# Five more Strassen groups, and the attention filled with parts of twenty of them

## The chip, the cores and the metric

The kernel runs on one core of one Trainium2 chip. Its time is that of the device for one execution, in microseconds (us). The core has a matrix engine (PE, with its weight loads shown as PEld), three engines for elementwise work (DVE, ACT and POOL) and a queue, SP, from which nearly all transfers are issued.

## What is computed

One layer of a hybrid backbone over 1024 tokens of 1024 channels. The normed and modulated input h is multiplied by one wide matrix; the columns of the product feed three branches, and each branch ends in a gate:

```python
z = h @ lp['w_in']                       # 1024 x 8704, used here from column 1536 on as 56 tiles of 128
ya = neighbourhood_attention(q, k, v, kc, vc, rpb) * silu(z[..., A_Z:B_B])
yb = bg * dw_conv(cg * val, w_conv3) * silu(gz)            # short convolution, 3 taps
u  = dw_conv(a * sigmoid(g), w_conv31) + b_conv            # 31 taps
yc = silu(layer_norm(u)) * silu(z[..., C_Z:GATES])
ga, gb, gc = split(sigmoid(z[..., GATES:]), 3)
m = ga * (ya @ w_out_a) + gb * (yb @ w_out_b) + gc * (yc @ w_out_c)
x = x + gate * (m @ w_o)
```

All is computed in float32 accuracy: each factor is split into a high and a low part, and a product takes three matmuls (high by high, high by low, low by high).

## The kernel before

Channels lie on the partitions, tokens on the free axis. A *channel tile* is 128 of the columns of z: `ZA`, `BG`, `CG`, `BV`, `BZ`, `CA`, `CGL`, `CZ` have four each, the gates `GT` twenty-four. h is kept split, as `hlf[half][k]`: eight rows k of 128 channels, two halves of 512 tokens, each with its high and low part. (`hcols` cuts columns from it.)

**A whole tile** (`plain`, lines 642 to 652) takes its weight row of 1024 in three pieces (`load_w`: a load on SP, a cast on ACT for the high part, a difference on POOL for the low part) and then 2 halves x 8 rows x 3 = 48 matmuls of 512 columns. ACT evicts the bank with a tanh (or, for a gate, a sigmoid); DVE makes the silu; a store takes it to DRAM.

**A Strassen group** (`group`, lines 803 to 836) makes two channel tiles at once with seven products instead of eight (Winograd's form): the weights of the two tiles are four blocks a11, a12, a21, a22 of 512 columns, h is four blocks B11, B12, B21, B22 (four rows by one half), and a product is 4 x 3 = 12 matmuls. Sums of weight blocks s1 to s4 are made on POOL (for the b groups partly on DVE, by `few`); the sums T1, T2, T3 and T4 of blocks of h are made in advance by `h_sums`, go through DRAM (`td`) and are loaded and split by `load_t`. T4 lies where B12 lay, in `hlf[1][0..3]`. The products in order are P1 = a11 B11 (bank ga), s2 T2 (gf), s1 T1 (gc), s3 T3 (gd), then a12 B21 added onto P1 in ga, which gives the first quarter C11 of the result, s4 B22 (ge), and a22 T4 added onto gd. DVE adds the products up: u2, v, then the quarters C22, C12, C21 (`add`). A bank to which a second product is added must first have been read. `run` interleaves: the last product of a group comes behind the first two products of the next.

**The long convolution** (`conv_steps`, lines 754 to 772) is done by DVE while PE makes the groups: 4 channel tiles x 31 taps x 2 halves, each tap a multiply-add of 512 columns onto a PSUM bank. `conv_step(n)` puts n taps at places in the groups (4 and 3 per group). After a tile's 31st tap ACT evicts it, and then the next tile's first tap may run.

**Order of the work.** The kernel names an order; a planner then walks the program with a model of the engines and puts on each engine's queue whatever is ready, what stands earlier in the program first. Each engine works its queue in that fixed order. `issue_after` forces an instruction behind another. Work that stands late in the program is so drawn forward to where PE waits for the attention.

The stages: the start and the first q, k, v (to about 110 us), the attention of eight heads (to 495 us) whose waits PE fills with q, k, v of the next heads, `glu` and then eight whole tiles (ZA and BZ, `plain`, lines 687 to 690); a bridge of two whole gate tiles after the attention's last product (lines 739 to 741) while the T blocks are loaded; 17 groups (to 845 us: four times b_start, a gate pair, b_end, then five of CZ and gates); `last_two`, two groups made together; then the merge of the branches (`merge`), the layer norm beside it, and the output product.

## Time and profile before

| | |
|---|---|
| median of 3 executions | 1102.34 us (1101.36 to 1103.52) |
| the profiled execution | 1105.51 us |
| its span, first to last instruction | 1103.6 us |
| PE busy | 1078.2 us, 5330 matmuls |
| DVE busy | 802.5 us |
| POOL busy | 628.0 us |
| ACT busy | 535.2 us |
| mean granted clock of PE | 0.99 |

Busy times are a union: overlapping instructions of an engine count once. Matmuls overlap, so the duration shown for one is longer than the time it adds. Rows of groups read: line, engine, operation, out<-in by the names of tiles, partitions x elements, count | busy us, mean ns of one | idle time of the engine before them and what ended it. Rows of windows give, for a stretch of the span, each engine's busy time with its number of instructions, then the granted clock, the share of the 16 DMA engines and GB/s.

### The profile page before, as it was taken

To read this page: it belongs to the slowest core of one execution; us is meant where nothing else is said; L and a number is where in the kernel's file an instruction comes from. 1 tells how busy PE (TensorE), PEld (TensorE's weight loads), DVE (VectorE), ACT (ScalarE), POOL (GpSimd) and SP (SyncE) were. 2 spreads that over 40 slices of the span, in tenths; PEclk is the share of its full clock that TensorE was granted. 3 is DMA by queue.
4 is the path that set the end of the run, shared out by engine and by line. 5 is a ranking of instruction groups with operands and counts; after the bars stand their busy time and mean duration, and the time that the engine had idled before them with its cause. 6 is when DMAs were issued, how large, how long until landed. Compare 5 with 4: busy or idle time off the path is not lost.

```text
span 1103.6 us, 15912 instructions
## 1 busy us (share of the span) xinstructions
PE 1078.2 (98%) x5330; PEld 923.4 (84%) x5330; DVE 802.5 (73%) x1379; ACT 535.2 (48%) x1138; POOL 628.0 (57%) x634
## 2 busy tenths in 40 slices
PE   6899999999999999999999999999999999999998
PEld 5788998998999888888888788888888888887886
DVE  6985577666766765536996898799794469889664
ACT  6765666667566655535223233333334344356630
POOL 3244967437536952213858677777778381493670
PEclk8899999999999999999999999999999999999999
DMA  9627523303213332119133433434344998372262
GB/s 350 220 77 249 179 60 117 111 34 104 94 66 86 108 122 77 63 43 352 34 130 105 135 114 119 149 106 163 123 143 177 375 363 303 120 244 77 96 223 101
DMA packets 79745, 163.17 MB, mean 148 GB/s; under 512 B 10320, under 2 KB 31440, under 8 KB 79568
## 3 DMA queue, kind: packets, MB, share of 16 engines
q1 hardware_dynamic: 75056, 160.06, 42.1%
q10 hardware_dynamic: 4608, 2.10, 0.7%
q8 instruction: 42, 0.69, 0.3%
q14 instruction: 39, 0.32, 0.1%
HBM read 120.18 MB, written 44.50 MB: 149 GB/s over the span
## 4 chain that ended last, share of the span: by engine, by line
PE 82%; POOL 6%; DMA 5%; issue 3%; DVE 1%; ACT 1%; SPq 1%; ACTq 0%; POOLq 0%; DVEq 0%
PE zaps L108 3%; PE zaps L109 3%; PE zaps L110 3%; PE py L609 3%; PE gd L791 3%; PE gd L793 3%; PE gd L792 3%; PE pp L589 3%; PE ga L791 3%; PE ga L793 3%; PE ga L792 3%; PE ps L108 3%; PE ps L110 3%; PE ps L109 3%; PE ops L108 3%
## 5 line engine op out<-in xcount | busy, mean ns | idle before, releaser
L767 DVE SCALAR_TENSOR_TENSOR cv<-upad,cf_t,cv 128x512 f32<-128x512 f32 x240 | 166.8, 744 | 0.1
L708 POOL TENSOR_TENSOR wl<-s,wh 128x512 fp32r<-128x512 f32 x69 | 93.3, 1364 | 15.9 <-ACT wh L707 15.1
L707 ACT CAST wh<-s 128x512 fp32r<-128x512 f32 x92 | 56.2, 617 | 92.4 <-POOL s L711 64.7
L91 POOL TENSOR_TENSOR wl<-wr,wh 128x384 fp32r<-128x384 f32 (+1 forms) x57 | 56.1, 992 | 72.2 <-ACT wh L89 61.5
L592 DVE TENSOR_TENSOR plo<-pp,phi 128x256 fp32r<-128x256 f32 (+2 forms) x96 | 54.3, 575 | 26.6 <-ACT phi L591 25.7
L708 POOL TENSOR_TENSOR wl<-wr,wh 128x512 fp32r<-128x512 f32 x44 | 60.8, 1382 | 4.3 <-ACT wh L707 4.2
L548 POOL TENSOR_TENSOR bias<-mk,img 64x96 f32<-64x96 bf16 (+1 forms) x96 | 45.8, 484 | 24.3 <-DVE mn L574 16.5
L591 ACT CAST phi<-pp 128x256 fp32r<-128x256 f32 (+2 forms) x96 | 46.4, 495 | 24.0 <-PE pp L589 23.4
L791 PE MATMUL ga<-ha,wh 128*128 128x512 f32 x148 | 57.6, 389 | 0.0
L792 PE MATMUL ga<-ha,wh 128*128 128x512 f32 x148 | 57.6, 389 | 0.0
L793 PE MATMUL ga<-ha,wl 128*128 128x512 f32 x148 | 57.6, 389 | 0.0
L575 ACT ACTIVATE pt<-sc,mn 128x256 f32<-128x256 f32 x64 | 30.5, 477 | 45.6 <-DVE mn L574 43.7
L574 DVE CUSTOM_DVE_ANT_0 pt<-sl,bias,mn 128x384 f32<-128x384 f32 (+1 forms) x64 | 37.2, 582 | 16.8 <-PE sl L571 15.7
L589 PE MATMUL pp<-ident,pt 128*128 128x128 f32 x304 | 47.0, 272 | 0.0
L79 POOL TENSOR_SCALAR ssh<-ssh 128x4 f32<-128x4 f32 (+1 forms) x40 | 11.4, 285 | 60.0 <-DVE ssh L228 57.2
L817 POOL TENSOR_TENSOR s<-wr 128x512 f32<-128x512 f32 x16 | 23.3, 1455 | 37.4 <-DMA wr<-in_wz 25.8
L89 ACT CAST wh<-wr 128x384 fp32r<-128x384 f32 (+1 forms) x66 | 31.4, 487 | 27.3 <-PE zaps L109 13.0
L589 PEld LDWEIGHTS pp<-ident,pt 128*128 128x128 f32 x304 | 38.0, 140 | 7.8
L978 ACT ACTIVATE c<-c 128x512 f32<-128x512 f32 x18 | 11.4, 632 | 63.9 <-DVE c L797 48.2
L708 POOL TENSOR_TENSOR wl<-wro,wh 128x512 fp32r<-128x512 f32 x12 | 17.1, 1428 | 42.5 <-ACT wh L707 31.4
L582 DVE TENSOR_SCALAR pt<-pt,mn 128x640 f32<-128x640 f32 (+1 forms) x64 | 40.0, 667 | 1.0
L80 POOL TENSOR_TENSOR ssh<-ssh,half_neg 128x4 f32<-128x4 f32 (+1 forms) x40 | 38.9, 974 | 3.0
(439 smaller groups left out, 3886.4 us busy)
## 6 DMA issues: line engine op xcount, KB each, us to landing
wr<-in_wz SPq DMA_DIRECT2D x34, 512.0 KB, 3.9
gs<-gd SPq DMA_DIRECT2D x24, 512.0 KB, 4.7
wada<-in_w_ada SPq DMA_DIRECT2D x16, 512.0 KB, 8.6
wrf<-in_wo SPq DMA_DIRECT2D x16, 512.0 KB, 3.6
cht<-chd SPq DMA_DIRECT2D x24, 256.0 KB, 3.2
wr<-in_wz SPq DMA_DIRECT2D x32, 192.0 KB, 2.4
wro<-in_wout SPq DMA_DIRECT2D x24, 256.0 KB, 5.3
gd<-gate SPq DMA_DIRECT2D x22, 256.0 KB, 3.3
```

The lines of the kernel that those rows point to most:

```text
L91: lo_eng.tensor_tensor(out=lo[:, :n], in0=raw[:, :n], in1=hi[:, :n].bitcast(F32), op=ALU.subtract)
L108: pe.matmul(ps, ah, bh, start=i == 0, stop=False)
L109: pe.matmul(ps, ah, bl, start=False, stop=False)
L110: pe.matmul(ps, al, bh, start=False, stop=i == n - 1)
L589: pe.transpose(out=pp[:, c * P : c * P + P], in_=src, identity=ident)
L592: dve.tensor_tensor(out=lo, in0=v, in1=hi.bitcast(F32), op=ALU.subtract)
L707: act.copy(hi, src)
L708: eng.tensor_tensor(out=lo, in0=src, in1=hi.bitcast(F32), op=ALU.subtract)
L767: dve.scalar_tensor_tensor(out=acc[b], in0=src, scalar=cf_t[:, i, j : j + 1], in1=acc[b], op0=ALU.mult, op1=ALU.add)
L791: pe.matmul(ps, wh, bh, start=first and j == 0, stop=False, skip_group_check=True)
L792: pe.matmul(ps, wh, bl, start=False, stop=False, skip_group_check=True)
L793: pe.matmul(ps, wl, bh, start=False, stop=last and j == 3, skip_group_check=True)
```

## The change

- `plain` is gone. The tiles ZA, BZ and the last two gates, ten in all, are now Strassen groups as well: a `plan` lists 22 groups (two BZ pairs, four b_start, four gate pairs, four b_end, two CZ pairs, two ZA pairs, four more gate pairs), before `last_two`.
- Of 20 of these (all but numbers 0 and 10) the two products on ga, P1 and a12 B21, are made ahead by `first_quarters`, with the whole weight row of the pair's first tile: 16 beside the attention, 4 in the bridge. P1 is copied out (`p1d`), then C11: as silu for ZA and BZ, raw into `gd` for gates (the sigmoid follows in `merge`), raw into `c11d` for the rest.
- In the group itself such a number loads P1 (and C11) and makes five products. Six conv taps stand in it, eight in a whole group.
- T4 is loaded and split beside the attention, before the fillers, into the place of B12, which no filler reads any more.
- A tap of the long convolution is one instruction of 1024 columns over two banks.
- ZA and BZ quarters made in groups get their silu from a sigmoid on ACT and a product on DVE (`twice_silu`).
- The loads and sums for group 0 (a BZ pair) are made early, with two splits ahead instead of one. Raw weight rows have four buffers instead of three. One product of b_end moves from DVE to POOL where C11 was made ahead.

```diff
+    plan = list(pairs())
+    whole_groups = (0, 10)
+    ahead_of = [n for n in range(len(plan)) if n not in whole_groups]
...
-        def plain(ct, dst, gate=False):
...
+        def quarter_part(part, n, w, ps):
+            for k in range(4 * part, 4 * part + 4):
+                wh, wl = w[k]
+                bh, bl = hcols(0, k, B512[0]), hcols(1, k, B512[0])
+                pe.matmul(ps, wh, bh, start=k == 0, stop=False, skip_group_check=True)
+                pe.matmul(ps, wh, bl, start=False, stop=False, skip_group_check=True)
+                pe.matmul(ps, wl, bh, start=False, stop=k % 4 == 3, skip_group_check=True)
+            kind, i, _ = plan[n]
+            t = tmp("quarter")
+            if part == 0:
+                p1d[n] = dst = dram.tile([P, 512], F32, name=f"p1d{n}")
+                act.copy(t, ps)
+            elif kind in ("za", "bz"):
+                dst = (zad if kind == "za" else zbd)[i][:, B512[0]]
+                act.activation(t, ps, AF.Tanh, scale=0.5)
+                dve.scalar_tensor_tensor(out=t, in0=t, scalar=1.0, in1=ps, op0=ALU.add, op1=ALU.mult)
+            else:
+                if kind == "gate":
+                    raw_gates.add(i)
+                    dst = gd[i][:, B512[0]]
+                else:
+                    c11d[n] = dst = dram.tile([P, 512], F32, name=f"c11d{n}")
+                act.copy(t, ps)
+            nc.sync.dma_start(dst, t)
...
-        for i in range(4):
-            plain(ZA + i, zad[i])
-        for i in range(4):
-            plain(BZ + i, zbd[i])
+        for j in range(4):
+            hi, lo = hcols(0, j, B512[1]), hcols(1, j, B512[1])
+            nc.sync.dma_start(lo.bitcast(F32), td[3][j])
+            act.copy(hi, lo.bitcast(F32))
+            dve.tensor_tensor(out=lo, in0=lo.bitcast(F32), in1=hi.bitcast(F32), op=ALU.subtract)
+        first_quarters(ahead_of[:-BEHIND])
...
     with tc.issue_after(state["py"].ins):
-        for i in (6, 7):
-            plain(GT + 2 * KT + i, gd[2 * KT + i], True)
+        first_quarters(ahead_of[-BEHIND:])
...
-            acc = [ps_c.tile([P, 512], F32, tag=f"cv{b}", name="cv") for b in range(2)]
+            acc = ps_c.tile([P, S], F32, tag="cv", name="cv")
             for j in range(31):
-                for b in range(2):
...
+                src = u[:, j : j + S]
...
+                    dve.scalar_tensor_tensor(out=acc, in0=src, scalar=cf_t[:, i, j : j + 1], in1=acc, op0=ALU.mult, op1=ALU.add)
...
+        if n is None:
+            a = bank("ga")
+            product(a, wa or wsplit(a11, pool), B11, True, True)
+            act.copy(p1, a)
+        else:
+            nc.sync.dma_start(p1, p1d[n])
+            if n in c11d:
+                c11 = tmp("c11")
+                nc.sync.dma_start(c11, c11d[n])
+                use0(0, c11)
...
-        conv_step(4)
-        product(a, wsplit(a12, pool), B21, False, True)
-        use0(0, a)
+        conv_step(3)
+        if n is None:
+            product(a, wsplit(a12, pool), B21, False, True)
+            use0(0, a)
+            conv_step(2)
...
-            (pool if b else dve).tensor_tensor(out=z, in0=t, in1=z, op=ALU.mult)
+            (pool if b or n in c11d else dve).tensor_tensor(out=z, in0=t, in1=z, op=ALU.mult)
...
+            if br * KT + dm in raw_gates:
+                act.activation(gs[:, :512], gs[:, :512], AF.Sigmoid)
```

More of the change, by code (lines that the diff above doesn't have):

```diff
@@ L126, in tile_hybrid, with pairs, lead @@
     B512 = [slice(0, 512), slice(512, 1024)]
+    p1d, c11d, raw_gates = {}, {}, set()
+    gate_no = [KT + k for k in range(KT)] + list(range(KT)) + [2 * KT + k for k in range(KT)]
+    def pairs():
+        g = iter(gate_no)
+        two_gates = lambda: ("gate", next(g), next(g))
+        for i in range(4):
+            if i % 2 == 0:
+                yield "bz", i, i + 1
+            yield "b_start", i, None
+            yield two_gates()
+            yield "b_end", i, next(g)
+        for i in range(4):
+            yield ("cz", i, i + 1) if i % 2 == 0 else ("za", i - 1, i)
+            yield two_gates()
+    plan = list(pairs())
+    whole_groups = (0, 10)
+    ahead_of = [n for n in range(len(plan)) if n not in whole_groups]
+    last_gates = gate_no[20:]
+    def lead(n):
+        kind, i, _ = plan[n]
+        return {"bz": BZ, "b_start": CG, "gate": GT, "b_end": BG, "cz": CZ, "za": ZA}[kind] + i
     state = {"wp": wp}
@@ L640, in attend, with quarter_bank @@
             nc.sync.dma_start(yad[hp], ya.rearrange("p r c -> p (r c)"))
-        def plain(ct, dst, gate=False):
-            w = load_w(wz[ct], KT, pool)
-            for b in range(2):
-                ps = ps_m.tile([P, 512], F32, tag="m", name="zaps")
-                mm3(ps, [(w[k][0], w[k][1], hcols(0, k, B512[b]), hcols(1, k, B512[b])) for k in range(KT)])
-                t = tmp("flt")
-                act.activation(t, ps, AF.Sigmoid if gate else AF.Tanh, scale=1.0 if gate else 0.5)
-                if not gate:
-                    dve.scalar_tensor_tensor(out=t, in0=t, scalar=1.0, in1=ps, op0=ALU.add, op1=ALU.mult)
-                nc.sync.dma_start(dst[:, B512[b]], t)
+        def quarter_bank():
+            state["qb"] = state.get("qb", 0) + 1
+            if state["qb"] % 3 == 0:
+                return ps_q.tile([P, 512], F32, tag="q", name="qps")
+            return ps_m.tile([P, 512], F32, tag="m", name="qps")
@@ L654, in h_sums, with first_quarters @@
+        def first_quarters(ns):
+            begun = None
+            for n in (*ns, None):
+                new = None
+                if n is not None:
+                    new = n, load_w(wz[lead(n)], KT, pool), quarter_bank()
+                    quarter_part(0, *new)
+                if begun:
+                    quarter_part(1, *begun)
+                begun = new
         def h_sums(j):
@@ L732, in tile_hybrid @@
     early = []
-    for ct in (CG, BV):
+    for ct in (BZ, BZ + 1):
         r = sp.tile([P, S], F32, tag="y", name="wry", bufs=2)
@@ L801, in ev, with raw_rows, group @@
         return sp.tile([P, 512], F32, tag="ev", name=name, bufs=4)
-    def group(ct0, ct1, use0, use1, few=pool, raw=None, w11=None):
+    def raw_rows():
+        state["wr"] = state.get("wr", 0) + 1
+        if state["wr"] % 4 == 0:
+            return sp.tile([P, D], F32, tag="wrs", name="wrs")
+        return wq.tile([P, D], F32, tag="wr", name="wr", bufs=3)
+    def group(ct0, ct1, use0, use1, few=pool, raw=None, sums=None, wa=None, wf=None, n=None):
         if not raw:
@@ L807, in group @@
             for ct in (ct0, ct1):
[L808 removed]
+                r = raw_rows()
                 nc.sync.dma_start(r, wz[ct])
@@ L964, in tile_hybrid, with run @@
     open_ = []
-    def run(*args):
-        g = group(*args)
+    def run(*args, **kw):
+        g = group(*args, **kw)
         next(g)
@@ L988, in zc_out, with twice_silu, use @@
         return use
-    gates = iter([KT + k for k in range(KT)] + list(range(KT)) + [2 * KT + k for k in range(KT - 2)])
-    def gate_pair():
-        i, j = next(gates), next(gates)
-        run(GT + i, GT + j, gate_out(i), gate_out(j))
+    def twice_silu(dst):
+        def use(b, t):
+            o = tmp("z2")
+            act.activation(o, t, AF.Sigmoid)
+            dve.scalar_tensor_tensor(out=o, in0=t, scalar=2.0, in1=o, op0=ALU.mult, op1=ALU.mult)
+            nc.sync.dma_start(dst[:, B512[b]], o)
+        return use
     def spill_split(t, i, b, eng):
@@ L1009, in meet @@
         def meet(b, t):
-            if b == 0 and b not in held:
+            if b == 0 and b not in held and n not in c11d:
                 c = tmp("c11")
```

76 lines of the change are left out of this document (42 added, 34 removed).

## The prediction

> **What bounds the kernel now.** I read the page's first part, then the busy times of each engine by stage, then PE's own waits, then the DVE and POOL groups of the Strassen stage.
>
> ```profile
> span 1103.6 us, 15912 instructions
> PE 1078.2 (98%) x5330; PEld 923.4 (84%) x5330; DVE 802.5 (73%) x1379; ACT 535.2 (48%) x1138; POOL 628.0 (57%) x634
> ```
>
> ```profile
> core 0: us, PE busy (x) PEld busy (x) DVE busy (x) ACT busy (x) POOL busy (x), PEclk, DMA share, GB/s
> ...
> 361.00:394.00 33.00, 33.00 (x173) 28.02 (x172) 25.85 (x42) 19.50 (x48) 31.40 (x31) 1.00 0.31 106
> 394.00:495.00 101.00, 101.00 (x523) 85.53 (x522) 50.70 (x113) 47.59 (x128) 21.27 (x26) 1.00 0.22 76
> 495.00:517.00 22.00, 22.00 (x99) 18.23 (x98) 11.93 (x18) 11.77 (x19) 3.88 (x9) 1.00 0.93 337
> 517.00:745.00 228.00, 225.97 (x990) 186.71 (x989) 203.93 (x273) 77.14 (x140) 173.94 (x135) 0.99 0.35 118
> 745.00:847.00 102.00, 102.00 (x451) 84.46 (x451) 86.92 (x128) 40.32 (x73) 79.32 (x62) 1.00 0.41 139
> ```
>
> The stages: the end of the attention (to 495), a bridge of filler products (to 517), the first twelve Strassen groups (to 745), the other five (to 845). PE has no idle time in four of these rows. From 745 to 847 it starts 451 matmuls of 512 columns in 102 us, so one takes **0.226 us**; the 0.39 us that the groups show as duration is overlap. The first twelve groups hold 12 x 84 = 1008 matmuls, 227.8 us at that rate, and took 228, a 2 us stall among them:
>
> ```profile
> PE gd L791 <- DVE c L797: 2.0, 1, 2.0
> ```
>
> With the restart after it (990 recorded matmuls at 0.226 are 223.9 of the 228 us, a few records missing) I put the stall at up to 4 us; 2 us is its idle time. So PE bounds the stage, but DVE is right behind it: 203.9 of 228 us.
>
> **What the change removes.** Two whole channel tiles are 2 x 48 = 96 matmuls; as a Strassen group they are 7 x 12 = 84. Five new groups save 60. The filler beside the attention stays 480: ten tiles of 48 before, twenty groups' first two products of 24 after. All 60 leave the Strassen stage: 17 x 84 = 1428 before, 20 x 60 + 2 x 84 = 1368 after, 60 x 0.226 = **-13.6 us** if PE goes on without waiting. The stall at 615 us goes or is contained in what follows: -4.0 at most, which I take, as the stall below is counted from no stall.
>
> [...]
>
> **DVE in the Strassen stage.** Its groups from 517 to 745, and two stretches of its timeline (start, us, what):
>
> ```profile
> L767 DVE SCALAR_TENSOR_TENSOR cv<-upad,cf_t,cv 128x512 f32<-128x512 f32 x160 | 111.5, 744 | 0.0
> L1025 DVE SCALAR_TENSOR_TENSOR by<-bu,cs_t,by 128x1024 f32<-128x1024 f32 x8 | 12.0, 1498 | 0.0
> L708 DVE TENSOR_TENSOR wl<-s,wh 128x512 fp32r<-128x512 f32 x12 | 12.0, 999 | 0.0
> L711 DVE TENSOR_TENSOR s<-wr,s 128x512 f32<-128x512 f32 x7 | 9.3, 1328 | 8.2 <-POOL s L711 8.2
> L708 DVE TENSOR_TENSOR wl<-wr,wh 128x512 fp32r<-128x512 f32 x7 | 8.8, 1254 | 4.6 <-ACT wh L707 4.6
> L822 DVE TENSOR_TENSOR u<-gf,p 128x512 f32<-128x512 f32 x12 | 8.2, 680 | 0.1
> L708 DVE TENSOR_TENSOR ysl<-zb,ysh 128x512 fp32r<-128x512 f32 x6 | 7.8, 1308 | 2.4 <-ACT ysh L707 2.4
> ...
> L708 DVE TENSOR_TENSOR hb<-hb 128x512 fp32r<-128x512 f32 x4 | 5.7, 1448 | 0.0
> L1023 DVE TENSOR_SCALAR by<-bu,cs_t 128x1024 f32<-128x1024 f32 x4 | 5.7, 1420 | 4.4 <-POOL bu L1015 4.4
> ```
>
> ```profile
> 652.89 0.68 DVE L797 TENSOR_TENSOR c<-gd,v 128x512 f32<-128x512 f32 x1
> 653.49 2.72 DVE L767 SCALAR_TENSOR_TENSOR cv<-upad,cf_t,cv 128x512 f32<-128x512 f32 x4
> 656.12 0.68 DVE L708 TENSOR_TENSOR wl<-s,wh 128x512 fp32r<-128x512 f32 x1
> ...
> 674.12 1.27 DVE L1025 SCALAR_TENSOR_TENSOR by<-bu,cs_t,by 128x1024 f32<-128x1024 f32 x1
> 675.32 1.40 DVE L767 SCALAR_TENSOR_TENSOR cv<-upad,cf_t,cv 128x512 f32<-128x512 f32 x2
> ```
>
> Instructions overlap by some 0.08 us, so what one costs is its distance to the next: four taps fill 2.63 us, **0.66** each; an add 0.60 (652.89 to 653.49); a 1024-wide tap over SBUF 1.20. No row shows a 1024-wide tap on PSUM. It lies between 1.20 (that SBUF row: as many elements through the same engine, so I see no reason for less) and 1.32 (two narrow ones, no gain; this end also holds the case that each tap waits for the full 1.27 of the one before, whose result it now reads at once, where two banks took turns before). I take 1.20, the row of the same width; the other end adds 88 x 0.12 = 10.6 us.
>
> The new order has 14 groups where 12 stood (two silu pairs, four b_start, four gate pairs, four b_end), 12 of them with five products and two whole: 12 x 60 + 2 x 84 = 888 matmuls, **200.9 us** of PE. DVE in them: taps 12 x 6 + 2 x 8 = 88 x 1.20 = 105.6; five adds a group, 70 x 0.60 = 42.0; the split of the last product 14 x 0.92 = 12.9; in the eight b groups one difference (1.25) and one split (1.17), 19.4; short conv 4 x 1.34 + 8 x 1.42 = 16.7; spill splits 8 x 1.23 = 9.8; seven silu products and one gate product, 8 x 0.60 = 4.8. The four T4 splits (5.7) are gone: they run beside the attention, under a DVE that is busy 50.7 of 101 us there. **Sum 211.2 us**, 10.3 more than PE's. (The same sum over the old stretch gives 203, and 203.9 was measured.) The groups after these have no short conv: 8 x 60 matmuls are 108.6 us of PE, against some 83 of DVE (36 taps 43.2, 40 adds 24, 8 splits 7.4, 14 silus 8.4). Over the whole stage DVE fits; in its first two thirds it does not, and the taps come in program order, so they can't all be put off.
>
> How much of that reaches PE depends on how far DVE may fall behind. The row to look at is the third product of a group, on whose bank the last product of the same group is added after DVE has read it:
>
> ```profile
> L793 PE MATMUL gd<-T,wl x4: 389/389/389, 643.7 to 645.8; 128*128 128x512 f32 x4
> L791 PEld LDWEIGHTS gd<-hb,wh x4: 187/188/188, 656.6 to 658.7; 128*128 128x128 f32 x4
> L797 DVE TENSOR_TENSOR c<-gd,v x1: 676/676/676, 652.9 to 652.9; 128x512 f32<-128x512 f32 x1
> ```
>
> The product ends at 646.2, DVE has read it at 653.6, **7.4 us** later, and PE comes back at 656.6: four products lie between (10.9 us). Now a five-product group has two between (5.4 us). So DVE, late by 7 us already, holds PE as soon as it is late by more than 5.4. I allow those 5.4 us once. To DVE's own time comes what it waits for POOL in order; of the 24 us idle from 517 to 745 I keep the 4.4 before the short conv (row above), since the others fell where the taps had run out for want of the next tile, and a DVE that is behind has taps left. Stall: 211.2 + 4.4 - 200.9 - 5.4 = **+9.3 us**; its ends are 0 (a deeper lag borne, as now) and 29 (all 24 us of idle kept).
>
> The wait itself: behind the DVE add stand the next taps and splits on DVE; behind PE's last product all of the next group, and the silu and gate evictions on ACT.
>
> [...]
>
> **POOL.** Per five-product group it has four splits and four sums, fewer in the b groups:
>
> ```profile
> L708 POOL TENSOR_TENSOR wl<-s,wh 128x512 fp32r<-128x512 f32 x38 | 51.7, 1372 | 12.4 <-ACT wh L707 11.6 <-POOL wl L708 0.8
> L817 POOL TENSOR_TENSOR s<-wr 128x512 f32<-128x512 f32 x12 | 17.7, 1472 | 22.3 <-DMA wr<-in_wz 14.9 <-PE gf L792 4.0 <-PE gf L793 3.4
> ```
>
> The 14 groups need 50 splits, 46 sums and 23 products of the b groups, 119 x 1.42 = 169 us of 201, where 174 lay in 228. PE covers that, if the inputs come in time; a fourth raw weight buffer works against the 14.9 us of waits on weights. Without that cover POOL would be level with PE at 1.69 us an operation.
>
> **Beside the attention.** Each group's two products need a weight row of its own, so twenty rows are loaded, cast and split instead of ten, and 40 banks are evicted instead of 20:
>
> ```profile
> L91 POOL TENSOR_TENSOR wl<-wr,wh 128x384 fp32r<-128x384 f32 x16 | 16.5, 1034 | 57.2 <-ACT wh L89 47.4 <-PE zaps L110 9.8
> L91 POOL TENSOR_TENSOR wl<-wr,wh 128x256 fp32r<-128x256 f32 x8 | 5.9, 737 | 6.1 <-ACT wh L89 6.1
> L649 ACT ACTIVATE flt<-zaps 128x512 f32<-128x512 f32 x15 | 8.9, 597 | 11.3 <-PE zaps L110 9.5 <-PE zaps L108 1.3 <-POOL wl L91 0.5
> ```
>
> A row costs POOL 2 x 1.03 + 0.74 = 2.8 us. From 394 on POOL is busy 21 of 101 us: room for all. From 361 to 394 it is busy 31.4 of 33, and the fillers that run there need about two rows more: 5.6 us against 1.6 free, so 4 us of filler may be late (ends: 0, if rows are split earlier; 4). ACT takes 16 evictions and 24 casts more, each at most 0.6: from 67 to at most 91 of 134 us, hidden. I take **+1**, nearer 0, since PE has attention products to run first. SP's queue takes 10 row loads (three pieces each) and 20 stores more; T4's four loads move from the groups to before the fillers. In the bridge the DMA share is 0.93; 1 MB more at 337 GB/s is 3 us late at most, and PE's 22.00 of 22 us show no wait, so 0. The 29 loads of finished quarters in the groups (7.6 MB in 310 us, 25 GB/s beside 118 to 139) hide under a DMA share of 0.35 to 0.41. Eight sigmoids of gate halves move to the merge, 8 x 0.6 on an ACT that is 48% busy: 0, or 4.8 if each held its product.
>
> **The sum.** -13.6 - 4.0 + 9.3 + 1.0 = **-7.3 us**. Against its own execution: span 1103.6 to 1096.3, and that execution's 1105.5 us to 1098.2. It stands 3.2 us above the median 1102.34; the same step from the median gives **1095**. Own range: 1089 to 1101.
>
> **Rivals.** (1) *PE stays the only bound*: DVE's lag is absorbed as now, when a 7.4 us lag cost nothing. For it: DVE's total over the stage fits; against it: 211 in 201. 1102.3 - 13.6 - 4.0 = 1085, with a few us of remainder 1086. (2) *The filler is late*: the full 4 us from 361 to 394 and the merge's ACT are paid: -7.3 + 3 + 4.8 = +0.5, 1103, no change. For it: POOL 31.4 of 33. Against: from 394 there is room. (3) *Slower: the shortened distance on the third product's bank.* DVE keeps all 24.1 us of its idle time, because at each conv tile's end the next tile waits for ACT's eviction (of both halves now), and PE, two products away, is held each time: 211.2 + 24.1 - 200.9 - 5.4 = 29, so -13.6 - 4.0 + 29 + 1 = +12.4, 1115. It decides from 12 us of idle on (stall above 16.6). For it: the one stall of the stage is this wait. Against: the idle time fell where DVE was ahead.
>
> **How the numbers follow.** Forecast 0.43, rival 1 0.25, rival 2 0.13, rival 3 0.19. From 1086 (rival 1) to 1108 (rival 3 with 17 of its 24 us of idle: a stall of 21.9, +5.3) lie about 8 in 10; it holds the wide tap's other end too (1095 + 10.6). A measurement of this kernel can't tell less than 0.2% (2.2 us) from no change. Faster: 0.43 x 0.9 + 0.25 + 0.13 x 0.3 = 0.68; same: 0.43 x 0.05 + 0.13 x 0.5 + 0.19 x 0.2 = 0.12; slower 0.20.
>
> **What would show it.** Right: 60 matmuls fewer; PE waits of some 9 us in all on DVE's read of the third product, in the first 14 groups only; DVE over 95% busy there; a wide tap every 1.20 us. Wrong: PE without waits (rival 1); waits on POOL's splits from 361 to 394 (rival 2); DVE idle over 12 us there while PE waits (rival 3); a wide tap at 1.28 or more.

## The result: slower, and the profile after

The changed kernel takes **1114.77 us** (median of 5, 1113.72 to 1117.16) against 1102.76 us of the kernel before on the same chip (median of 5): a ratio of 1.011, 95% interval 1.009 to 1.0129. That is 12 us slower where 7 us faster was forecast, and outside the range of 1086 to 1108. The profiled execution took 1117.16 us, its span is 1115.4 us.

The first part of the page of the changed kernel, and one row of its groups (busy us, mean ns of one | idle before them and what ended it):

```profile
span 1115.4 us, 16056 instructions
PE 1069.6 (96%) x5270; PEld 909.8 (82%) x5270; DVE 813.9 (73%) x1283; ACT 556.0 (50%) x1181; POOL 682.4 (61%) x676
...
L830 DVE SCALAR_TENSOR_TENSOR cv<-upad,cf_t,cv 128x1024 f32<-128x1024 f32 x120 | 153.4, 1278 | 0.6
```

The 60 matmuls are gone (5330 before, 5270 now). In their place PE waits 19.6 us for line 860, DVE's read of a group's third product. That wait was 2.0 us before. It comes in 14 pieces, ten in the first fourteen groups and four in the other eight; the row of PE's own waits (us in total, times, longest):

```profile
PE gd L854 <- DVE c L860: 19.6, 14, 3.1
```

Where the time lies can be read off three marks on the timelines (start, us, what): the first half of the fifth of the attention's eight outputs (`ya`), the first matmul of the groups, the start of what follows the last group. First before, then after:

```profile
335.29 0.68 DVE L639 TENSOR_TENSOR ya<-py,ya 64x512 f32<-64x512 f32 x1 [1.82 <-ACT ya L638]
...
516.97 0.39 PE L791 MATMUL ga<-ha,ah 128*128 128x512 f32 x1
...
844.55 0.39 PE L791 MATMUL gc<-T,wh 128*128 128x512 f32 x1
```

```profile
336.02 0.68 DVE L666 TENSOR_TENSOR ya<-py,ya 64x512 f32<-64x512 f32 x1 [1.82 <-ACT ya L665]
...
522.32 0.39 PE L854 MATMUL ga<-ha,ah 128*128 128x512 f32 x1
...
856.19 0.39 PE L854 MATMUL gd<-hb,wh 128*128 128x512 f32 x1
```

(In the changed kernel one product of `last_two` is drawn ahead of the last group's last one, so the start of that one is the mark that compares.) From these marks:

| stretch | before | after | difference |
|---|---|---|---|
| to the fifth output | 335.3 | 336.0 | +0.7 |
| fifth output to the first group | 181.7 | 186.3 | **+4.6** |
| the groups | 327.6 | 333.9 | **+6.3** |
| last_two, merge, output | 259.1 | 259.2 | +0.1 |

The groups' matmuls take 323.4 us before (1428 x 0.2265) and 309.8 us now (1368); 0.2265 us lies between the 0.2262 of 451 matmuls in 102 us and the 0.2267 of twelve starts in 2.72 us. So they lost 4.2 us to waits before and lose **24.1** now. The windows of the changed kernel answer to the prediction's; 522.4 to 742 are its first fourteen groups, 742 to 856 the other eight:

```profile
361.00:394.00 33.00, 31.86 (x163) 26.32 (x163) 23.78 (x39) 20.75 (x50) 31.92 (x28) 1.00 0.42 144
394.00:500.00 106.00, 104.68 (x535) 87.05 (x534) 49.79 (x109) 67.53 (x174) 48.05 (x55) 1.00 0.47 154
500.00:522.40 22.40, 22.40 (x100) 18.31 (x99) 10.33 (x16) 13.78 (x25) 6.57 (x13) 1.00 0.98 353
522.40:742.00 219.60, 205.39 (x894) 166.56 (x892) 206.21 (x211) 68.48 (x119) 186.44 (x140) 1.00 0.50 168
742.00:856.00 114.00, 108.62 (x474) 88.61 (x475) 97.33 (x105) 42.21 (x73) 94.84 (x69) 1.00 0.50 170
```

The fourteen groups took 219.6 us. The 894 matmuls in that row are 202.5 us. DVE is busy 206.2 us there, 94%; it idles for 13.4. DVE's timeline shows the two ways in which the read of line 860 (`c<-gd,v`) comes late. In the ninth group the third product's last matmul starts at 654.7 and ends at 655.1; the read is done at 663.4, with no idle time in between:

```profile
L856 PE MATMUL gd<-T,wl x4: 389/389/389, 652.6 to 654.7; 128*128 128x512 f32 x4
```

```profile
654.99 2.60 DVE L830 SCALAR_TENSOR_TENSOR cv<-upad,cf_t,cv 128x1024 f32<-128x1024 f32 x2
657.50 0.68 DVE L860 TENSOR_TENSOR c<-gd,u 128x512 f32<-128x512 f32 x1
658.10 1.17 DVE L771 TENSOR_TENSOR s<-wr,s 128x512 f32<-128x512 f32 x1
659.19 0.68 DVE L768 TENSOR_TENSOR wl<-s,wh 128x512 fp32r<-128x512 f32 x1
659.79 0.68 DVE L907 TENSOR_TENSOR v<-gc,u 128x512 f32<-128x512 f32 x1
660.40 1.27 DVE L830 SCALAR_TENSOR_TENSOR cv<-upad,cf_t,cv 128x1024 f32<-128x1024 f32 x1
661.59 1.24 DVE L1076 SCALAR_TENSOR_TENSOR z<-c,z 128x512 f32<-128x512 f32 x1
662.74 0.68 DVE L860 TENSOR_TENSOR c<-gd,v 128x512 f32<-128x512 f32 x1
...
```

In the sixth group the product ended at 610.6, and DVE stood idle: the short convolution (line 1110), ahead of the read in DVE's fixed order, waited for POOL:

```profile
L856 PE MATMUL gd<-T,wl x4: 389/389/389, 608.2 to 610.2; 128*128 128x512 f32 x4
```

```profile
609.29 0.69 DVE L907 TENSOR_TENSOR v<-gc,u 128x512 f32<-128x512 f32 x1
615.48 1.77 DVE L1110 TENSOR_SCALAR by<-bu,cs_t 128x1024 f32<-128x1024 f32 x1 [5.49 <-POOL bu L1099]
617.17 1.28 DVE L830 SCALAR_TENSOR_TENSOR cv<-upad,cf_t,cv 128x1024 f32<-128x1024 f32 x1
618.36 0.68 DVE L860 TENSOR_TENSOR c<-gd,v 128x512 f32<-128x512 f32 x1
```

The lag from the product's end to the end of the read was as long before: 7.1 to 9.3 us in ten of the first twelve groups, and PE was ready to write the bank again 10.3 to 10.9 us behind the product, so that only a lag of 12.8 us, in the fifth group, cost a wait, of 2.0 us. Now the lags of the first fourteen groups are 4.5 to 8.7 us, but PE is ready again after 5.4 to 8.0 us: two products lie between, three in two groups, and in places up to eight matmuls that the planner drew ahead. Counted group by group on the timelines, PE's wait is the lag less this distance, to 0.15 us, in all 22 groups.

### The profile page after: what moved, and what is told of

Read it like the earlier page. It is cut to its first block, busy times and chain, and to the rows that moved or that the text cites. A ratio compares the mean times of both kernels' runs of the same rounds, so it can differ in the third digit from the quotient of the medians.

```text
span 1115.4 us, 16056 instructions
## 1 busy us (share of the span) xinstructions
PE 1069.6 (96%) x5270; PEld 909.8 (82%) x5270; DVE 813.9 (73%) x1283; ACT 556.0 (50%) x1181; POOL 682.4 (61%) x676
## 5 line engine op out<-in xcount | busy, mean ns | idle before, releaser
L830 DVE SCALAR_TENSOR_TENSOR cv<-upad,cf_t,cv 128x1024 f32<-128x1024 f32 x120 | 153.4, 1278 | 0.6
L92 POOL TENSOR_TENSOR wl<-wr,wh 128x384 fp32r<-128x384 f32 (+1 forms) x87 | 86.0, 995 | 71.4 <-ACT wh L90 53.1
L768 POOL TENSOR_TENSOR wl<-s,wh 128x512 fp32r<-128x512 f32 x83 | 120.3, 1452 | 14.2 <-ACT wh L767 13.4
L767 ACT CAST wh<-s 128x512 fp32r<-128x512 f32 x111 | 66.8, 616 | 96.7 <-POOL s L771 41.5
L90 ACT CAST wh<-wr 128x384 fp32r<-128x384 f32 (+1 forms) x96 | 45.8, 483 | 40.5 <-PE qps L680 21.4
L679 PE MATMUL qps<-ha,wh 128*128 128x512 f32 x160 | 63.7, 399 | 0.0
L681 PE MATMUL qps<-ha,wl 128*128 128x512 f32 x160 | 63.5, 397 | 0.0
L680 PE MATMUL qps<-ha,wh 128*128 128x512 f32 x160 | 63.0, 394 | 0.0
L854 PE MATMUL gd<-hb,wh 128*128 128x512 f32 x96 | 39.1, 407 | 19.6 <-DVE c L860 19.6
L601 DVE CUSTOM_DVE_ANT_0 pt<-sl,bias,mn 128x384 f32<-128x384 f32 (+1 forms) x64 | 37.2, 581 | 15.8 <-PE sl L598 14.8
L854 PEld LDWEIGHTS gd<-hb,wh 128*128 128x128 f32 x96 | 18.0, 187 | 29.1 <-DVE c L860 23.1
L109 PE MATMUL ps<-wh,hb 128*128 128x384 f32 x112 | 38.9, 347 | 0.8 <-ACT rawc L224 0.5
```

The source lines that it names most:

```text
L92: lo_eng.tensor_tensor(out=lo[:, :n], in0=raw[:, :n], in1=hi[:, :n].bitcast(F32), op=ALU.subtract)
L109: pe.matmul(ps, ah, bh, start=i == 0, stop=False)
L679: pe.matmul(ps, wh, bh, start=k == 0, stop=False, skip_group_check=True)
L680: pe.matmul(ps, wh, bl, start=False, stop=False, skip_group_check=True)
L681: pe.matmul(ps, wl, bh, start=False, stop=k % 4 == 3, skip_group_check=True)
L767: act.copy(hi, src)
```

## The experiments

The theories for the groups: DVE has too much **work**; DVE's in-order waits for POOL, the **links**, make the read late; the shortened **distance** between read and write. For the attention: the copies of the **T4** step on ACT, or the **doubled rows**. "To first group" is the stretch from the fifth output. All runs are given with the lengths of the stretches of the table above, read off in the same way, and PE's wait for the third product's read:

| kernel | time, us | ratio to before | to first group | groups | rest | wait |
|---|---|---|---|---|---|---|
| before | 1102.8 | 1 | 181.7 | 327.6 | 259.1 | 2.0 |
| changed | 1114.8 | 1.0110 | 186.3 | 333.9 | 259.2 | 19.6 |
| one tap of 31 | 1106.0 | | 186.1 | 325.6 | 259.3 | 11.1 |
| distance | 1113.7 | 1.0097 | 186.5 | 333.7 | 258.9 | 14.3 |
| narrow taps | 1119.2 | 1.0150 | 186.7 | 335.7 | 259.2 | 18.0 |
| T4 later in the program | 1117.6 | 1.0134 | 186.9 | 332.9 | 259.2 | 15.0 |
| short conv. behind the read | 1114.7 | 1.0112 | 184.3 | 334.0 | 258.9 | 14.8 |
| one tap, links cut | 1107.0 | | 185.2 | 316.5 | 269.4 | 4.5 |
| taps by kind | 1115.0 | 1.0111 | 184.4 | 333.5 | 258.1 | 15.7 |
| T4 forced later | 1114.6 | 1.0110 | 186.2 | 334.6 | 259.0 | 16.2 |
| by kind, forced | 1112.3 | 1.0081 | 185.2 | 336.4 | 257.8 | 18.2 |
| + links cut | 1108.2 | 1.0045 | 185.3 | 321.4 | 263.6 | 7.3 |
| + distance instead | 1107.5 | 1.0038 | 185.8 | 326.8 | 258.5 | 10.0 |
| links and distance | 1114.5 | 1.0106 | 186.0 | 328.6 | 263.6 | 9.7 |
| six rows on DVE | 1116.6 | 1.0117 | 184.8 | 336.6 | 259.1 | 16.8 |
| six rows on DVE, T4 forced | 1116.8 | 1.0130 | 184.6 | 336.3 | 258.9 | 16.2 |
| links, distance, six rows, T4 forced | 1112.3 | 1.0086 | 184.4 | 327.5 | 263.0 | 10.7 |
| sums behind six rows | 1120.8 | 1.0165 | 193.3 | 331.9 | 259.0 | 16.2 |
| links cut alone | 1121.2 | 1.0167 | 186.2 | 328.6 | 269.6 | 13.7 |
| before, wide taps | 1104.1 | 1.0013 | 181.7 | | | 2.2 |

The stretches come from one profiled execution each, the times from all; intervals are about 0.0015 to either side (0.004 for T4 later in the program). The two kernels with one tap were timed in one execution each. The profiled execution lies between 2.1 us below its kernel's median (taps by kind) and 2.9 above it (by kind, forced), so stretches that differ by 2 or 3 us show no difference. In the kernels with the distance joined up to six more matmuls of `last_two` stand ahead of the last mark, which makes their groups up to 1.4 us longer and the rest shorter.

**One tap of 31.**

```diff
-            for j in range(31):
+            for j in range(1):
```

> The changed kernel with one of the 31 taps of the long convolution; the other thirty are left out, so VectorE loses 120 wide operations, about 86 of them (105 us) in the first fourteen groups. If VectorE's lag is what holds the matrix products, PE's wait of 19.6 us for the read of the third product is under 3 us and the kernel takes 1095 to 1099. If the rows' splits on POOL (186 us busy of 219.6 there) stand behind the lag, over 10 of the 19.6 us stay and the time is over 1106.

Eleven of the 19.6 us stay, and the second expectation held in all but 0.04 us: taking nearly all taps away saves 8.3 us in the groups, not 20. DVE's waits from 520 to 860 of this run, and POOL's:

```profile
DVE ysl L768 <- ACT ysh L767: 25.2, 6, 7.8
DVE u L902 <- DMA p<-p1d: 19.9, 7, 5.6
DVE by L1110 <- POOL bu L1099: 13.5, 3, 5.7
```

```profile
POOL s L885 <- DMA wr<-in_wz: 13.6, 6, 4.2
...
POOL s L885 <- DMA wrs<-in_wz: 11.7, 7, 3.9
```

DVE had little to do, and still seven reads ended 5.6 to 8.6 us behind their product. Between product and read it stood idle 11.3 us for the spilled low parts (`ysl`, whose input comes from POOL over ACT) and 7.4 us for the short convolution, which stand ahead of the read; of the waits for P1's loads, the second row, only 0.1 us lies there. POOL in its turn waits for raw weight rows, whose buffers come free late: in the changed kernel, from 522 to 856, SP waited before such loads 33.3 us for sums on POOL and 31.1 us for sums on DVE. So work alone is not the cause.

**The distance.** In the group, the first `yield`, at which the last product of the group before is issued, moves from behind `u2` to behind `v`, and `ev` has five buffers.

> The last product of the group before is moved behind the next group's second product, so that three products and not two lie between the third product's read and the write into the same bank (about 8.1 us and not 5.4; one more buffer for evictions). Distance theory: VectorE's lag of 7 to 8.7 us then mostly fits, PE's wait for that read falls from 19.6 to under 6, the fourteen groups take 206 to 211 us and not 219.6, and the kernel takes 1102 to 1107. Throughput theory (VectorE alone sets the pace of these groups): the wait stays or grows as VectorE falls further behind, and the time is 1111 to 1116.

The time (1113.7) is the throughput theory's; the wait did not stay or grow, as that theory had it, but fell to 14.3 us, in six pieces of up to 5.3. PE was now ready again after 8.0 to 8.2 us in most groups. The taps stood before the reads as in the changed kernel (8, 8, 6 and 5 up to the fourth read, there 8, 8, 6 and 4); PE waited less at first, and DVE's lag grew to 11.9 us in the fourth group with no idle time between product and read, and to 13.4 in the twelfth. Distance alone brings nothing.

**The price of the wide tap.** The old form, two instructions on two banks:

```diff
-            acc = ps_c.tile([P, S], F32, tag="cv", name="cv")
+            acc = [ps_c.tile([P, 512], F32, tag=f"cv{b}", name="cv") for b in range(2)]
```

> The changed kernel with the taps of the kernel before: two of 512 elements in two banks in place of one of 1024. By the price on which the prediction stood (1.20 against 1.32 us for the two) 88 taps more cost VectorE 10.6 us, and where VectorE sets the pace of the fourteen groups the kernel takes 1121 to 1126. By the trace's rows of taps that follow taps directly (1.28 to 1.32 us each) the wide form brings 0 to 3.5 us: 1114 to 1119.

1119.2, just above the second expectation and below the first, 4.4 us above the changed kernel by the ratios (1.015 to 1.011). The taps' row of DVE in the first fourteen groups, wide and then narrow:

```profile
L830 DVE SCALAR_TENSOR_TENSOR cv<-upad,cf_t,cv 128x1024 f32<-128x1024 f32 x81 | 103.5, 1278 | 0.5
```

```profile
L831 DVE SCALAR_TENSOR_TENSOR cv<-upad,cf_t,cv 128x512 f32<-128x512 f32 x158 | 110.5, 743 | 0.0
```

By busy time a wide tap is 1.28 us and a pair of narrow ones 110.5 / 79 = 1.40. Both hold the end that overlaps the next instruction. From one start to the next without idle time, as the prediction counts, the timelines give 1.21 on the mean for a wide tap and 0.66 for a narrow one: a saving of 0.11 a tap, near the forecast 0.12.

> The kernel before with the wide taps alone, one of 1024 elements over two banks in place of two of 512. In the changed kernel the wide form was worth 4.4 us against the narrow one, where VectorE's lag holds the matrix products. In the kernel before only one wait of 2.0 us stands behind VectorE's lag, with some 1.7 us of slow matrix products behind it: theory of VectorE's work: that one goes at most, 1098 to 1103. If a tap that follows a tap directly is no faster in the wide form and the lag stays: 1102 to 1105. If both halves of a tile now waiting for one eviction cost more: above 1105.

The kernel before with this edit alone: 1.0013, interval 1.0004 to 1.0022. The time, 1104.1, is the second expectation's: in this kernel the wide form is worth nothing, and the wait it was to remove is there still (2.2 us).

**T4.** Its load moved back behind the first group, first by its place in the program only, then with its start forced behind that group's first eviction.

> The fourth pre-added block is loaded and split behind the first group again, as before, and not beside the attention. If that step's copies on ScalarE, which wait for its transfers with the attention's copies behind them, make the attention's loss of 4.7 us, at most 1.5 us of it are left; the four splits cost the first groups up to 4 us, so the time is 1110 to 1116. If the doubled row splits of the filler make the loss, 3 us or more of it stay and the time is 1114 to 1119.

> The fourth block's load and split forced behind the first group's first eviction (loaded late in the program alone it was drawn forward to the same place beside the attention). If its copies, waiting for transfers ahead of the attention's own on ScalarE, make the attention's loss, the last attention output and the first group come 3 to 5 us earlier, and the kernel takes 1110 to 1115 with the splits in the first groups. If the doubled rows make it, the first group starts within 1.5 us of the changed kernel's, and the time is 1114 to 1119.

The first came out no different and decides nothing: with the buffers free the planner drew the loads to the same place, and ACT waits for them there, from 361 to 420, as in the changed kernel (4.5 us):

```profile
ACT hb L762 <- DMA hb<-td: 6.1, 4, 2.7
```

The second was moved: 186.2 us to the first group, as in the changed kernel, though T4 is gone from there, and a time in the second expectation's range (1114.6). T4 alone is not the cause.

**The short convolution behind the read; one tap with the links cut.** The edits: lines 1110 to 1112 under `issue_after` of the last read; in the second kernel also

```diff
-            spill_split(z, i, b, dve)
+            spill_split(z, i, b, pool)
...
-        return wq.tile([P, D], F32, tag="wr", name="wr", bufs=3)
+        return wq.tile([P, D], F32, tag="wr", name="wr", bufs=4)
```

and, for room, seven buffers instead of eight for `wl`.

> The three instructions of the short convolution are forced behind the third product's read of the group that runs then, so that this read no longer stands behind VectorE's wait for POOL (6.2 us in two waits in the changed kernel, 13.5 us in three with one tap). Theory of the chain (VectorE's in-order waits for POOL make the read late): 4 to 8 us of PE's 19.6 go, 1107 to 1111. Throughput theory: VectorE's work stays, the lag stays, 1113 to 1117.

> One of 31 taps as before (thirty are left out), and three links from VectorE to POOL cut as well: the short convolution forced behind the third product's read, the low parts of the spilled results made on POOL and not on VectorE, and a buffer more for raw weight rows. With one tap alone 11.1 us of PE's wait for that read stayed. Theory of the chain: under 3 us stay and the kernel takes 1092 to 1098. If something else holds the read (PE's own order, the distance), 8 us or more stay: 1103 to 1107.

With the taps in place, forcing the short convolution back brings nothing (groups 334.0), and the time, 1114.7, is the second expectation's. DVE's idle time in the first fourteen groups did not fall: 12.9 us up to the start of the groups' 889th matmul, 12.5 in the changed kernel up to the same mark. It waited 2.6 us for POOL before the short convolution where it had waited 6.2, and 4.9 us for loads of P1. With the taps out and all three links cut, the groups take 316.5 us, 17.4 less than in the changed kernel and 6.7 from PE's own 309.8; the wait is 4.5 us. So work and links together account for 17.4 of the 24.1 us that the stage loses. The wait missed both expectations (under 3 us, 8 us or more); the time, 1107.0, is in the second one's range only because 10 us were lost later:

```profile
PE ops L109 <- DVE ops L771: 7.3, 1, 7.3
```

This wait in the merge is 0.6 us in the changed kernel. It is larger in every kernel with the two edits shown and the seven buffers (7.3, 2.6, 3.2, 3.2, 7.3), and I did not separate the three.

**Taps dealt out by kind.** `conv_step` gets counts by the kind of the group; in the second kernel each batch is forced behind the read ahead of it, and the short convolution too.

> All taps, dealt out by what else VectorE has in a group: 3 where a short convolution and spills stand, 5 in the groups that start one, 7 in gate groups, 6 in the rest, 11 in the first, so that some 70 and not 88 lie in the first fourteen groups and some 54 and not 36 in the last eight. Throughput theory: VectorE's work in the first fourteen falls by some 22 us below PE's, PE's wait there falls under 8 us, and the time is 1102 to 1108 (the last eight lose up to 4). Theory of the chain: the waits for POOL stay as with one tap, 11 us of the wait stay, and the time is 1106 to 1112.

> Taps dealt out by kind as before, but now each batch is forced behind the third product's read after which it stands (dealt out alone they were drawn forward: 73 of them still lay in the first fourteen groups, nine in the first), and the short convolution behind that read as well. Theory of two causes (VectorE's work and its in-order waits for POOL, either enough by itself to hold the read): with both eased PE's wait falls under 10 us, the first fourteen groups take 207 to 214 us and not 219.8, the time is 1102 to 1110. If VectorE's work alone counts, 1100 to 1106; if neither, 1112 to 1117.

Neither helped the groups (333.5, 336.4), and the times, 1115.0 and 1112.3, miss the first one's expectations and meet the "neither" of the second. The first still had some 72 taps in the first fourteen groups, of 84. In the second it was 68, and DVE was busy 193.7 us there instead of 204.6 (both up to the 889th matmul), yet PE waited 18.2 us. Work alone is refuted a second time, and my theory that these two edits would do was wrong as well. In eight of the fourteen groups one to three taps still lie between product and read, and what DVE waited for longest is not one of the links I had named but the loads of P1: 10.7 of its 23.8 idle us in the first fourteen groups (the row counts from 518 to 890):

```profile
DVE u L906 <- DMA p<-p1d: 11.8, 5, 4.9
```

**Joined.**

> The changed kernel with the three links from VectorE to POOL cut (short convolution behind the third product's read, spilled low parts on POOL, a buffer more for raw rows) and the taps left as they were dealt. With the taps dealt out as well, 1108.2 and a wait of 7.3 us. Theory of two causes, either enough by itself: VectorE's work holds the read as before, the wait is over 11 us and the time 1110 to 1115. If the links were the whole cause, the wait is under 9 us and the time 1106 to 1110.

> The same, with the other two links from VectorE to POOL cut too: the low parts of the spilled results on POOL, and a buffer more for raw weight rows (one fewer for the low parts of the groups' weights). Theory of two causes: the first fourteen groups take 203 to 210 us, PE's wait is under 6 us, the time is 1098 to 1106, and no merge stall as in the run with three links cut. If POOL, which has the eight splits more, is the bound by now: the wait moves to products waiting for POOL's splits and the time is 1106 to 1115.

> The same as the first of these, with the last product of the group before moved behind the next group's second product, so that three products lie between read and write. Moved alone this brought nothing in the first fourteen groups, as VectorE fell further behind. Distance theory joined to it: with VectorE's work evened out its lag of up to 8 us fits in 8.1 us, PE's wait is under 3 us, the first fourteen take 203 to 208 us, the time is 1098 to 1105. If VectorE falls behind without end in the groups with short convolutions, the wait stays over 8 us and the time is 1106 to 1114.

> Taps by kind and forced, the short convolution behind the third product's read, the spilled low parts on POOL, the buffer more for raw rows (one fewer for high and low parts of the groups' weights), and three products instead of two between read and write. Theory of three causes that add (VectorE's work, its waits for POOL, the distance): the wait, 7.3 us with the links cut and 10.0 with the distance, falls under 3 us, the first fourteen groups take 203 to 208 us, the time is 1101 to 1106; what is left over the kernel before is then the attention's 4 us. If cutting links and lengthening the distance take away the same waits, the wait stays at 6 us or more and the time is 1106 to 1109.

Links cut alone: groups 328.6, 5.3 less than in the changed kernel. Taps dealt out and forced: 336.4. Both: **321.4**, 12.5 less. That is what two causes look like that cover for each other, but it does not separate them: the links' edit also takes the eight spill splits, 8 x 1.13 us, from DVE to POOL, and is so a cut of work as well. Only the kernels with one tap, where DVE has time to spare, show the links by themselves (325.6 to 316.5). Taps dealt out and the distance: 326.8, 7.1 less, where the distance alone brought 0.2. That edit brings a fifth `ev` buffer, into which P1 is loaded too, and with it DVE's wait for P1 is gone; no run has the distance without the buffer, so which of the two helped is not shown. All three together did worse (328.6) than either pair, against my expectation; there are six waits as with the links cut, but up to 3.5 us long where they were 2.4 at most, and behind the longest PE's matmuls started 0.427 us apart for a while (below). No combination reaches 309.8, and none is faster than the kernel before.

Held against the expectations: with the links cut alone the wait, 13.7 us, is the two-cause theory's, but the time, 1121.2, is above both ranges, as 10.4 us went in the merge. With both (7.3 us, 1108.2) the first fourteen groups took 208.3 us, in the two-cause theory's range; its wait and its time are missed narrowly. The time is in the other theory's range without its mark, since PE did not wait for POOL's splits. Taps and distance (10.0 us, 1107.5) fall under the second expectation. All three (9.7 us) keep the second one's wait, at a time, 1114.5, above both ranges.

**Beside the attention.** The low parts of the first six filler rows on DVE, alone and with T4 forced; then POOL's last sums placed behind six filler rows; then all edits.

> The changed kernel with the low parts of the first six weight rows beside the attention made on VectorE and not on POOL. If POOL (31.9 us busy of 33 from 361 to 394) is what delays the fillers and with them the attention, the first group starts 2 to 4 us sooner after the sixth attention output and the time is 1110 to 1113. If it is ScalarE, whose casts of the doubled rows wait in order for their transfers with the attention's casts behind them, nothing changes: 1114 to 1117, or later by VectorE's added work.

> The changed kernel with the first six rows' low parts on VectorE and the fourth block forced behind the first group's first eviction. Each alone moved a part of the attention's loss but not the sum: with the rows on VectorE the loss between 60 and 75 us after the fifth output went and that before it stayed, with the block moved it was the other way about. If two things share ScalarE's queue there (the block's copies and the casts that wait for POOL or for transfers), both together leave at most 2 us of 4.5: first group 182 to 184 us behind the fifth attention output (186.3 in the changed kernel, 181.7 before), time 1110 to 1114. If it is the number of casts and transfers itself, 185 to 187 and 1113 to 1118.

> The changed kernel with the last two calls of the sums of h on POOL placed behind the first six filler rows, so that the rows' splits go first. If POOL, full from 361 to 394, delays the rows and so the fillers, the first group starts 182 to 184 us behind the fifth attention output and the time is 1110 to 1113. If not, 185 to 188 us and 1113 to 1118.

> All edits of the two kernels above together. If the two losses are independent, the time is the first one's less what the second gains over the changed kernel, 1098 to 1103, not slower than the kernel before. If the attention's loss is not mended, 1102 to 1107.

The six rows alone bring the first group 1.5 us nearer and the time nothing (1116.6, the second expectation). The 1.5 us are no finding either: the kernels whose edits lie in the groups alone have their first group at 184.3 to 186.7 us. With T4 forced as well PE has no idle time from 361 to 500 (1.14 and 1.32 us in the changed kernel's windows above):

```profile
361.00:394.00 33.00, 33.00 (x173) 27.97 (x172) 29.69 (x47) 18.98 (x44) 25.60 (x23) 1.00 0.56 186
394.00:500.00 106.00, 106.00 (x545) 89.68 (x544) 49.44 (x108) 66.81 (x171) 40.43 (x49) 1.00 0.47 156
```

The attention's last product came 7.1 us sooner (157.0 us behind the fifth output, 164.1 in the changed kernel and 161.9 to 164.9 in every kernel without both edits but that with later sums, 159.2 in the kernel before). So the two edits together remove the loss there: POOL full of splits and sums (31.9 of 33 us), and ACT's copies waiting in order (4.5 us for T4); what each weighs is not shown. But the first group came only 1.7 us sooner, and the time (1116.8) is the second expectation's: 108 filler matmuls instead of 96 are then left for the bridge, which waits there for POOL (`qps L681 <- POOL wl L92`, 1.9 us). With POOL's sums later the attention's last product came at 152.4 us, but 157 filler matmuls were left behind it and the first group came 7 us later still: that expectation failed both ways. All edits together (1112.3) are 2.2 us better than links and distance alone and still slower than before; the second expectation's range too was missed.

## Why the prediction was wrong, point by point

- **60 matmuls, -13.6 us**: right. With DVE relieved the last eight groups took the forecast 108.6 us in the runs with one tap, and in the changed kernel the matmuls of the stage are 13.6 us fewer. All of it was given back.
- **DVE's work, 211.2 us in fourteen groups**: right to 1%. DVE was busy 206.2 us up to 742. Of what the prediction counted it had then done 84 of 88 taps (81 in the row above, and three tiles' first), 68 of 70 adds and seven of eight spill splits, as the rows below and those of `u` and `v` (14 each) show. At the prediction's prices the remainder is 4 x 1.20 + 2 x 0.60 + 1.23 = 7.2 us, together 213.4. The price of a tap was right too: 1.21 us on the mean from start to start, against 1.20. The 1.28 in its row is the duration, so the text's own sign of being wrong, a tap at 1.28, was not seen in the way the prediction counted.

```profile
L860 DVE TENSOR_TENSOR c<-gd,v 128x512 f32<-128x512 f32 x14 | 9.5, 678 | 0.0
L860 DVE TENSOR_TENSOR c<-gd,u 128x512 f32<-128x512 f32 x13 | 8.8, 681 | 0.0
L860 DVE TENSOR_TENSOR c<-ge,v 128x512 f32<-128x512 f32 x13 | 8.8, 678 | 0.0
L768 DVE TENSOR_TENSOR ysl<-zb,ysh 128x512 fp32r<-128x512 f32 x7 | 8.5, 1207 | 2.7 <-ACT ysh L767 2.6
```

- **The stall, +9.3**: the step that failed, by its term for DVE's idle time. That PE is held as soon as DVE is later than the distance was right, group by group. But the 219.6 us of the stretch hold 202.5 us of matmuls, a stall of 17.1 us, 7.8 more than forecast. In the forecast's terms that is +2.2 for DVE's work, -1.8 for the lag (7.2 us of work carried out of the stretch, where 5.4 was allowed), -1.6 for the 894 matmuls instead of 888, and **+9.0** for idle time: 13.4 us where 4.4 was kept. What ended DVE's idle times in the first fourteen groups:

```profile
DVE by L1110 <- POOL bu L1099: 6.2, 2, 5.5
DVE ysl L768 <- ACT ysh L767: 2.6, 2, 1.3
DVE u L902 <- PE gd L855: 2.0, 1, 2.0
DVE cv L828 <- DMA upad<-ud: 1.2, 1, 1.2
DVE cv L828 <- ACT cvo L834: 0.8, 1, 0.8
```

  "A DVE that is behind has taps left" failed: it had taps left, but in a fixed order it did not take them while the short convolution at the head of its queue waited for POOL (5.5 us, in the timeline of the sixth group). This is a sum of times. It does not say that PE gains what one such wait is cut by: with the short convolution forced back the idle time moved elsewhere, and with all taps the groups became over 6 us shorter only where edits were joined.
- **The groups after, 0**: the second step that failed. 114.0 us for the 474 matmuls of their row, 107.4 us: another 6.6. The text set 83 us of DVE against 108.6 of PE there, but DVE brought 7.2 us of work into them. In the first of them the read came 10.3 us behind its product, and the last of the waits lies in the twentieth group, where the taps run out.
- **The attention, +1**: measured +4.6. The bounds were set from POOL alone (0 to 4); ACT was called hidden by its busy time, and it waits in order for transfers there (4.5 us for T4's and 4.4 us for weight rows from 361 to 420). Undoing either alone left the first group where other edits put it too; undoing both brought the attention's end 7.1 us forward, and the loss went into the bridge and the groups.
- **Bridge and merge, 0**: right in the changed kernel (22.4 us without a wait; rest 259.2 against 259.1).
- **Rivals**: the time is that of the third, 1115, and its mark, DVE idle over 12 us while PE waits, was seen (13.4). Its reason was only half right: most of the idle time came from POOL's links (6.2 and 2.6 us), little from the ends of conv tiles (2.0 us), and it was 13 us, not 24. That the number fits is luck: its stall of 29 us in the first fourteen groups was 17.1, and the 6.6 us of the last eight and the attention's 3.6, which it did not have, made up for most of that. The first rival is refuted; of the second, the attention's 3.6 us above my +1 are a part. The 19.8 us between forecast and result are so 14.6 in the groups (-8.3 forecast, +6.3 measured), 3.6 beside the attention and 1.6 elsewhere: 0.8 in the other stretches, the remainder from setting medians beside profiled executions.
- **The prices of DVE's other instructions** were taken from rows of before, and POOL is denser now (186.4 us busy of 219.6, 173.9 of 228 before). Of the three rows of the fourteen groups the first is longer than its 999 ns of before, the others are shorter than their 1498 and 1328. These are means over all such instructions.

```profile
L768 DVE TENSOR_TENSOR wl<-s,wh 128x512 fp32r<-128x512 f32 x15 | 17.1, 1143 | 0.6 <-ACT wh L767 0.6
L1112 DVE SCALAR_TENSOR_TENSOR by<-bu,cs_t,by 128x1024 f32<-128x1024 f32 x8 | 11.4, 1431 | 0.0
L771 DVE TENSOR_TENSOR s<-wr,s 128x512 f32<-128x512 f32 x8 | 10.2, 1272 | 0.0
```

What stays open: which of the three edits makes the merge wait, whether the distance or its fifth buffer helped, why distance and links together are worse than either, and the 11.6 us that the groups still lose in the best kernel with all taps.

## What to carry to other kernels

A lag that costs nothing now only fits the present distance (here 7.1 to 9.3 us fitted the 10.3 to 10.9 of before, and 4.5 to 8.7 did not always fit the 5.4 to 8.0 of now): before shortening the distance between a read and the write behind it, compare the lag with the new distance, group by group. An engine that is behind can still stand idle (DVE 5.5 us behind POOL, in the sixth group): where it works in a fixed order, read who stands at the head of its queue and whom that one waits for, rather than setting busy time against the other engine's. What it carries out of one stretch (7.2 us here) is work in the next. Where two causes each suffice to make something late, removing one shows little, so remove both before ruling either out.

## What the runs showed of the hardware

**Behind a wide tap the next tap started later than another operation did.** In the changed kernel's timeline of the ninth group a wide tap with another operation behind it gave way after 1.19 us (660.40 to 661.59), while two in a row took 2.51 (654.99 to 657.50): 1.32 for the one followed by its own successor, which is its duration of 1.27 and a little more. That successor reads what the tap wrote, in the same banks; no run separates the two. In the first fourteen groups 13 taps had a tap behind them and 69 another operation, so the mean stayed near the price I had taken.

**Behind some of its waits PE ran at half clock.** In the run with links and distance, behind a wait of 3.5 us, matmuls started every 0.427 us instead of 0.227, fourteen of them. PE's timeline there, and then windows, whose third column from the right is the granted clock:

```profile
735.36 0.63 PE L857 MATMUL gd<-hb,wl 128*128 128x512 f32 x1
735.78 0.63 PE L855 MATMUL gd<-hb,wh 128*128 128x512 f32 x1
```

```profile
734.00:738.00 4.00, 3.63 (x9) 2.89 (x10) 3.80 (x5) 2.18 (x4) 4.00 (x4) 0.50 0.40 108
738.00:742.00 4.00, 4.00 (x14) 3.20 (x13) 0.00 (x0) 0.41 (x1) 4.00 (x4) 0.71 0.84 283
742.00:746.00 4.00, 4.00 (x19) 3.29 (x19) 3.69 (x5) 2.50 (x5) 4.00 (x4) 1.00 0.27 85
```

That is 2.9 us on top of the wait. Eight such matmuls, 1.7 us, followed the single 2.0 us wait of the kernel before, while none followed the fourteen waits of the changed kernel, the longest of which is 3.1 us. The granted clock behind the one (0.57) and behind that longest wait of the other (1.00):

```profile
617.00:621.00 4.00, 3.92 (x10) 3.16 (x11) 4.00 (x6) 1.11 (x2) 2.75 (x4) 0.57 0.37 142
```

```profile
759.80:763.00 3.20, 3.20 (x14) 2.62 (x15) 3.20 (x4) 1.75 (x3) 2.35 (x2) 1.00 0.65 209
```

The granted clock of 0.50 stands where the matmuls start 0.427 us apart. With taps dealt out and the distance, PE waited 4.5 us, and the granted clock behind it, from 736.5 to 740, was 0.50 as well. So a wait of 2.0 us had a slow stretch behind it and one of 3.1 us had none: the length alone did not decide, and what did is not shown.
